# The last half tile of a matmul–GELU–matmul kernel stored in three pieces instead of two

## The chip, the cores and the metric

The kernel runs on one core of one Trainium2 chip. A core has five engines that run their own instruction streams: PE (TensorE, matrix products), DVE (VectorE), ACT (ScalarE), POOL (GpSimd) and SP (SyncE), and 16 DMA engines that move data between HBM and the on-chip memory. Engines wait for each other and for transfers through semaphores. The metric is device time in microseconds (us), from repeated runs; a profile shows one execution, instruction by instruction.

## What is computed

```python
m, k, n, p = 1024, 1024, 2048, 1024        # a: m x k, b: k x n, c: n x p, all float32

def reference(a, b, c):
    h = np.matmul(a, b)
    h = 0.5 * h * (1 + np.tanh(np.sqrt(2 / np.pi) * (h + 0.044715 * h ** 3)))
    return np.matmul(h, c).astype(np.float32)
```

## The kernel before

The products are made in tiles of 128 rows by 512 columns; one such float32 result fills one of the eight PSUM banks. Inputs are cast to bf16. The first product fills `hT` (the GELU of `a @ b`, transposed), partly with plain products and partly with a scheme of seven products in place of eight (a Strassen–Winograd form, class `Seven`, function `seven`); the sums that this scheme needs are made by DVE and kept in float32r. The second product, `h @ c`, is the call `seven(two, done2, between2)`: the output's 8 row tiles by 2 column halves are 16 tiles of 128x512, and each is stored as soon as it is complete.

The order of all instructions is written out by hand (`manual_schedule`): each engine runs its instructions in the order in which the program issues them. What matters here is the end of `seven` for `two`:

- The three output tiles (0,0,j), j = 0 to 2, are finished early, after the second group of products. `done2` stores them; those with j = 1 and j = 2 are stored in two halves of 256 columns each (line 436), the one with j = 0 whole.
- Then come the tiles (1,1,j) and (0,1,j) (function `p3`) and (1,0,j) (function `p4`; DVE copies these out of PSUM on line 434). Each is one store of 128x512, 256 KB.
- The tile (0,0,3) was left over: its first part `p1[3]` has lain in SBUF since the start of this stage, and its second product is made last of all, in lines 368 to 376. It is made in two halves of 256 columns. For each half, PE runs 8 matmuls (`w.product`, line 212, each with its own weight load) into a bank of its own (`bank(PY[i])`, where `PY` is `(7, 4, 5, 6)`), DVE adds `p1[3]` (line 375) into a piece `ot` of the pool "e", which has two buffers, and `store` (line 429) sends it to HBM.
- All stores and the five first loads are issued on SP's queue; the casting loads are issued on POOL's. ACT issues no transfer at all.

Transfers issued on hardware queues (SP's, and ACT's if it were used) take eight semaphores in turn, and each waits until the transfer eight places earlier has landed. There are 5 loads and 19 stores, 24 in all. After the last store is issued, SP waits for the eight semaphores one after the other, and a barrier of all engines ends the program.

Of the kernel before, what the change touches and what calls it, by code (L numbers as in the profile page):

```python
# [9 lines left out]
F32 = mybir.dt.float32  # L10
# [9 lines left out]
def kernel(ctx, tc, a, b, c, out):  # L20
    nc = tc.nc
# [21 lines left out]
    def bank(i, shape=(128, H), dt=F32, name="ps"):  # L43
        return pp.tile(list(shape), dt, name=name, tag=f"bank{i}", padded_shape=None)

    def pieces(tag, bufs, shape, dt, name):
        return small.tile(shape, dt, name=name, tag=tag, bufs=bufs)
# [248 lines left out]
    def snap(tag, p, name):  # L296
        st = pieces(tag, 4, [128, H], F32, name)
        nc.scalar.activation(st, p, AF.Copy)  # L298
        return st

    def plus(p, st):
        ot = pieces("o", 4, [128, H], F32, "ot")
        nc.vector.tensor_tensor(out=ot, in0=p, in1=st, op=ADD)  # L303
        return ot

    def seven(w, done, between):

        (A11, A12), (A21, A22) = w.A
        (B11, B12), (B21, B22) = w.B
        J = range(w.n)  # L310
        PX = X[:w.n]
        P2, PY = (X[2:], Y[:2]) if w.n == 2 else (Y, Y)
        if w is two:
            PY = (7, 4, 5, 6)
        px = [bank(i) for i in PX]
        p1, v, u, p2 = {}, {}, {}, []
        for j in J:
            w.product(px[j], A11, B11, j, True)
            if w is two and j == 3:
                p1[j] = pieces("ab", 2, [128, H], F32, "p1")  # L320
                nc.scalar.activation(p1[j], px[j], AF.Copy)
            else:
                p1[j] = snap("m", px[j], "p1")
        between("P1")
        for j in J if w is not two else range(3):
            p = bank(P2[j])
            w.product(p, A12, B21, j, True)
            if w.n == 2:
                p2.append(p)
            else:  # L330
                done(0, 0, j, plus(p, p1[j]))
        between("P2")
        py = [bank(i) for i in PY]
        for j in J:
            w.product(py[j], w.s[0], w.t[0], j, True)
        between("P5")
        for j in J:
            w.product(px[j], w.s[1], w.t[1], j, False)
            v[j] = snap("v", px[j], "v")
        between("P6")  # L340
        c22 = []
        for j in J:
            w.product(px[j], w.s[2], w.t[2], j, False)
            u[j] = snap("m", px[j], "u")
            c22.append(plus(py[j], u[j]))
            between(f"P7{j}")

        def p3(first):
            for j in J:
                if first:  # L350
                    done(1, 1, j, c22[j])
                w.product(py[j], w.last_s, w.t[3], j, False)
                done(0, 1, j, plus(py[j], v[j]))
            between("P3")

        def p4(first):
            for j in J:
                if first:
                    done(1, 1, j, c22[j])
                w.product(px[j], w.s[3], w.last_t, j, False)  # L360
                done(1, 0, j, px[j])

        for i, f in enumerate((p4, p3) if w.n == 2 else (p3, p4)):
            f(i == 0)
            if i == 0:
                for j, p in enumerate(p2):
                    done(0, 0, j, plus(p, p1[j]))
        if w is two:

            for i in range(2):  # L370
                r = ds(i * 256, 256)
                p = bank(PY[i])
                w.product(p, A12, B21, 3, True, i * 256, 256)
                ot = pieces("e", 2, [128, 256], F32, "ot")
                nc.vector.tensor_tensor(out=ot, in0=p[:, r], in1=p1[3][:, r], op=ADD)  # L375
                store(3, i * 256, 256, ot)


    two = Seven(8, [[hT[0][:, 0:8], hT[0][:, 8:16]], [hT[1][:, 0:8], hT[1][:, 8:16]]],
# [35 lines left out]
    zero.s1()  # L415
    zero.s2()
    seven(zero, done0, between0)
    one.s[3] = slot("b1", [128, 2, 4, H], F32R, "x1")[:, 0]
    one.s1()
    one.s2()  # L420
    seven(one, done1, between1)


# [4 lines left out]
    def store(mt, q0, w, ot, eng=None):  # L428
        (eng or nc.sync).dma_start(out=out[ts(mt, 128), ds(q0, w)], in_=ot)

    def done2(i, l, j, p):
        if (i, l) == (1, 0):
            ot = pieces("o", 4, [128, H], F32, "ot")
            nc.vector.tensor_copy(ot, p)
            p = ot
        n = 2 if (i, l) == (0, 0) and j else 1
        for q in range(n):
            r = ds(q * (H // n), H // n)
            store(4 * i + j, l * H + q * (H // n), H // n, p[:, r])

    def between2(n):
# [12 lines left out]
        elif n == "P73":  # L454
            two.t4(two.t[1], 4)

    seven(two, done2, between2)


# [28 lines left out]
```

## Time and profile before

| what | value |
|---|---|
| median of 3 runs | 117.73 us (117.45 to 117.9) |
| span of the profiled execution, first to last instruction | 115.67 us, granted TensorE clock 1.000 |
| own time of the profiled execution | not listed separately; the runs' median is 2.06 us above the span |
| PE, DVE, ACT, POOL busy | 111.1, 90.0, 51.4, 17.2 us |
| last instruction of PE / of DVE's arithmetic | ends at 112.4 / 112.9 us |
| last store issued on SP | 112.90 us |
| stores issued on SP's queue | 19 of `ot`: 13 of 256 KB, 6 of 128 KB |

Times in a timeline are counted from the span's start. A line of the timeline gives the start, the length, the engine, the line of the kernel, the operation, its tiles as output<-input, the shape, how many instructions were merged, and in brackets how long the engine had been idle and what ended that. "SPq" is SP's sequencer issuing a transfer; the transfer itself runs later on the DMA engines. A matmul's length contains its way through the array, so that successive matmuls overlap; the distance between their starts is what each one costs. "To landing" is the time from the start of an issue to the last semaphore update of that transfer.

### The profile page before, as it was taken

How to read it: one execution, taken by the hardware profiler on the slowest of the kernel's cores; microseconds unless marked ns; L12 is line 12 of the kernel's file. 1: busy time of each engine (PE TensorE's matmuls, PEld its weight loads, DVE VectorE, ACT ScalarE, POOL GpSimd, SP SyncE). 2: the span in 40 equal slices, each digit the busy share in tenths (PEclk: the TensorE clock that was granted, in tenths of full speed). 3: DMA queues.
4: the chain of work that ended last, by engine and by line, in shares of the span. 5: the costliest groups of instructions: out<-in, count | busy, mean ns of one | idle time of the engine just before them, and what ended most of it. 6: DMA issues, size and time to landing. Idle time of an engine off the chain costs nothing.

```text
span 115.7 us, 1461 instructions
## 1 busy us (share of the span) xinstructions
PE 111.1 (96%) x542; PEld 77.1 (67%) x542; DVE 90.0 (78%) x107; ACT 51.4 (44%) x86; POOL 17.2 (15%) x29
## 2 busy tenths in 40 slices
PE   7989999999999999999999999999999999999980
PEld 6645555546776447888885444688888888888860
DVE  0347748789999998935699999999999986954770
ACT  5053000999259997166698429500124982000000
POOL 2497755223322000000000000000000000000000
PEclk9999999999999999999999999999999999999999
DMA  2999999999999999998000000060000002014993
GB/s 69 295 381 229 200 199 205 204 208 205 206 211 209 212 213 209 212 210 168 8 0 0 6 0 0 38 235 0 0 0 0 0 4 91 1 73 176 370 363 106
DMA packets 13414, 15.94 MB, mean 138 GB/s; under 512 B 736, under 2 KB 9312, under 8 KB 13408
## 3 DMA queue, kind: packets, MB, share of 16 engines
q0 software_dynamic: 8672, 9.31, 47.6%
q1 hardware_dynamic: 4736, 6.56, 15.8%
q8 instruction: 4, 0.07, 0.3%
q14 instruction: 2, 0.02, 0.0%
HBM read 20.97 MB, written 4.19 MB: 218 GB/s over the span
## 4 chain that ended last, share of the span: by engine, by line
PE 90%; DMA 5%; SPq 1%; DVE 1%; issue 0%
PE ps L212 76%; PE ps L114 11%; DMA sta<-in_a_dram 5%; PE pt L145 3%; SPq L76 0%; DVE ab L110 0%; SPq L75 0%; DVE ot L375 0%
## 5 line engine op out<-in xcount | busy, mean ns | idle before, releaser
L212 PE MATMUL ps<-x,s 128*128 128x512 f32 x128 | 29.6, 391 | 0.0
L212 PEld LDWEIGHTS ps<-x,s 128*128 128x128 f32 x128 | 24.0, 188 | 5.1
L212 PE MATMUL ps<-x,x 128*128 128x512 f32 x96 | 22.9, 394 | 0.0
L212 PEld LDWEIGHTS ps<-x,x 128*128 128x128 f32 x96 | 18.0, 188 | 3.9
L114 PE MATMUL ps<-aT,b 128*128 128x512 bf16 x64 | 16.1, 379 | 0.2 <-DVE b L110 0.2
L298 ACT ACTIVATE v<-ps 128x512 f32<-128x512 f32 x10 | 6.0, 599 | 19.1 <-PE ps L212 19.1
L212 PE MATMUL ps<-c_sb,hT 128*128 128x512 bf16 (+1 forms) x72 | 14.2, 356 | 0.0
L212 PE MATMUL ps<-x 128*128 128x512 f32 x56 | 13.2, 392 | 0.0
L212 PEld LDWEIGHTS ps<-x 128*128 128x128 f32 x56 | 10.2, 188 | 2.6 <-ACT u L298 0.4
L118 ACT ACTIVATE hT<-ps 128x512 bf16<-128x512 f32 x14 | 7.3, 595 | 9.7 <-PE ps L114 9.7
L212 PEld LDWEIGHTS <-hT 128*128 128x128 bf16 x72 | 6.9, 98 | 7.0 <-issue 0.5
L118 ACT ACTIVATE hT<-ot 128x512 bf16<-128x512 f32 x18 | 10.4, 624 | 2.0 <-DVE ot L303 2.0
L212 PE MATMUL ps<-aT,b 128*128 128x512 bf16 x48 | 10.7, 379 | 0.0
L146 DVE COPY aT<-pt 128x512 bf16<-128x512 bf16 x16 | 6.7, 423 | 5.1 <-PE pt L145 5.1
L303 DVE TENSOR_TENSOR ot<-ps,u 128x512 f32<-128x512 f32 x10 | 6.7, 690 | 5.1 <-ACT u L298 5.1
L303 DVE TENSOR_TENSOR ot<-ps,v 128x512 f32<-128x512 f32 x10 | 6.7, 688 | 4.8 <-DMA out_dram<-ot 3.8
L170 DVE TENSOR_TENSOR x<-c_sb 128x1024 fp32r<-128x1024 bf16 x8 | 9.3, 1226 | 0.0
L114 PEld LDWEIGHTS <-b 128*128 128x128 bf16 x64 | 5.7, 98 | 4.5 <-DVE b L110 0.3
L212 PEld LDWEIGHTS <-b 128*128 128x128 bf16 x48 | 4.6, 98 | 5.7 <-issue 0.3
L104 POOL DMA_DIRECT2D c_sb<-in_c_dram x8 | 5.6, 702 | 13.1 <-DMA b<-in_b_dram 12.4
L170 DVE TENSOR_TENSOR x<-b 128x1024 fp32r<-128x1024 bf16 (+1 forms) x4 | 7.0, 1752 | 0.6 <-issue 0.6
L298 ACT ACTIVATE u<-ps 128x512 f32<-128x512 f32 x10 | 5.9, 598 | 3.4 <-PE ps L212 3.2
(44 smaller groups left out, 111.3 us busy)
## 6 DMA issues: line engine op xcount, KB each, us to landing
c_sb<-in_c_dram POOLq DMA_DIRECT2D x8, 512.0 KB, 20.0
out_dram<-ot SPq DMA_DIRECT2D x13, 256.0 KB, 2.1
b<-in_b_dram POOLq DMA_DIRECT2D x6, 512.0 KB, 15.3
sta<-in_a_dram SPq DMA_DIRECT2D x3, 512.0 KB, 6.1
abq<-in_a_dram POOLq DMA_DIRECT2D x5, 256.0 KB, 7.9
out_dram<-ot SPq DMA_DIRECT2D x6, 128.0 KB, 2.0
stb<-in_b_dram SPq DMA_DIRECT2D x1, 512.0 KB, 5.3
b<-in_b_dram POOLq DMA_DIRECT2D x2, 256.0 KB, 8.2
```

Of the source, the lines that this page charges most:

```text
L104: nc.gpsimd.dma_start(out=c_sb[:, t:t + 2], in_=cv[:, t:t + 2])
L114: nc.tensor.matmul(p, b1[:, k, ts(t, 128)], aT[:, h, k], start=(k == 0), stop=(k == KT - 1))
L118: nc.scalar.activation(hT[h][:, t], p, AF.Gelu_apprx_tanh)
L145: nc.tensor.transpose(pt[:, n, ts(m, 128)], ab[:, m, ts(n, 128)], ident)
L146: nc.vector.tensor_copy(aT[:, h, 2 * q + n], pt[:, n])
L170: nc.vector.tensor_tensor(out=dst[:, r], in0=x[:, r], in1=y[:, r], op=op)
L212: nc.tensor.matmul(p[:, ds(c0, w)], l[:, k, ts(j, 128)], r[:, k, ds(c0, w)], start=(start and k == 0), stop=(k == self.kt - 1), skip_group ...
L298: nc.scalar.activation(st, p, AF.Copy)
L303: nc.vector.tensor_tensor(out=ot, in0=p, in1=st, op=ADD)
```

## The change

The last half tile's second half is cut into two pieces of 128 columns. The pieces are now 256, 128 and 128 columns wide, each with 8 matmuls into a bank of its own (7, 4 and 5), one DVE addition and one store. The pool "e" gets a third buffer. The first piece's store is issued on ACT's queue, the other two on SP's. The early tile (0,0,2) is stored whole, so that there are still 24 transfers on the hardware queues (5 loads, 19 stores).

```diff
         if w is two:
-            for i in range(2):
-                r = ds(i * 256, 256)
+            for i, (c0, n) in enumerate(((0, 256), (256, 128), (384, 128))):
+                r = ds(c0, n)
                 p = bank(PY[i])
-                w.product(p, A12, B21, 3, True, i * 256, 256)
-                ot = pieces("e", 2, [128, 256], F32, "ot")
+                w.product(p, A12, B21, 3, True, c0, n)
+                ot = pieces("e", 3, [128, 256], F32, "ot")[:, 0:n]
                 nc.vector.tensor_tensor(out=ot, in0=p[:, r], in1=p1[3][:, r], op=ADD)
-                store(3, i * 256, 256, ot)
+                store(3, c0, n, ot, nc.sync if i else nc.scalar)
...
-        n = 2 if (i, l) == (0, 0) and j else 1
+        n = 2 if (i, l, j) == (0, 0, 1) else 1
         for q in range(n):
             r = ds(q * (H // n), H // n)
             store(4 * i + j, l * H + q * (H // n), H // n, p[:, r])
```

## The prediction

> **What bounds the kernel now.** I read the busy shares first, then the chain of waits, then the last microseconds line by line, since the change touches only those and one early store. From the page and the chain in order of time:
>
> ```profile
> PE 111.1 (96%) x542; PEld 77.1 (67%) x542; DVE 90.0 (78%) x107; ACT 51.4 (44%) x86; POOL 17.2 (15%) x29
> ...
> 24.46 87.96 PE ps L212 x400
> 112.42 0.02 issue
> 112.44 0.42 DVE ot L375
> ```
>
> PE is busy without a hole to 112.4 us; one DVE addition follows. From there on no engine computes, yet the span goes on to 115.7: a tail of 3.3 us of which the chain, which ends at the last computing instruction, shows only the beginning. The timeline of the end:
>
> ```profile
> 110.49 1.92 PE L212 MATMUL ps<-c_sb,hT 128*128 128x256 bf16 x16
> 110.68 0.69 DVE L434 COPY ot<-ps 128x512 f32<-128x512 f32 x1 [0.21 <-PE ps L212]
> 111.57 0.42 DVE L375 TENSOR_TENSOR ot<-ps,p 128x256 f32<-128x256 f32 x1 [0.20 <-PE ps L212]
> 112.44 0.42 DVE L375 TENSOR_TENSOR ot<-ps,p 128x256 f32<-128x256 f32 x1 [0.45 <-PE ps L212]
> ...
> 112.02 0.33 SPq L429 DMA_DIRECT2D out_dram<-ot  x1
> 112.90 0.33 SPq L429 DMA_DIRECT2D out_dram<-ot  x1
> ```
>
> Each addition starts some 0.04 us after its last matmul, each store some 0.03 us after its addition. The issues in the window from 111 us take this long to land, and the DMA engines' busy tenths from 113 to 114 and from 114 to 115 us (slices of 25 ns) show where the last one's data move:
>
> ```profile
> DMA to landing us min/median/max: 1.9/1.9/2.0
> ...
> DMA  9898999977441000000000000000053997999899
> ...
> DMA  9948541000000000000000000000000000000000
> ```
>
> The second burst is the last store: it begins in the slice at 113.73, 0.83 us after the issue, moves for 0.45 us to 114.18, and lands at about 112.90 + 1.88 = 114.78 (1.9 in the row, 1.88 by its last semaphore update). The barrier takes 115.67 - 114.78 = 0.89 us more. So the tail is: PE ends 112.41; addition to 112.87; issue 112.90; start 0.83; data 0.45; landing 0.60; barrier 0.89.
>
> **The change, part by part.**
>
> *PE.* Eight matmuls of 256 columns become sixteen of 128, with eight more weight loads. The old ones start every (1.92 - 0.27)/15 = 0.110 us (0.273 is the length of one), eight take 0.88. The new shape stands in the trace, with a weight load of the same shape before each: the transposes.
>
> ```profile
> 8.38 0.62 PE L145 MATMUL pt<-ident,ab 128*128 128x128 bf16 x8
> L145 PE MATMUL pt<-ident,ab 128*128 128x128 bf16 x24 | 2.2, 219 | 0.4 <-DVE aT L146 0.2
> ```
>
> (0.62 - 0.22)/7 = 0.057 us apart, sixteen 0.91. So +0.03 at most; from below 0 (the streamed columns are the same). I take +0.02. The Trainium skill, "TensorE: Matmul & The Clock Gate", section "Back-to-back issue gap", speaks against the change: it gives about 81 ns per matmul for a stream of load-and-multiply pairs at 128 columns. By that figure the sixteen would take an estimated 1.30 us, 0.42 more than now, and the sum below would end some 0.2 above the time before. This case's rows have 57 ns for such pairs, so the measurement decides. The third piece's bank was last read by the third addition of line 303, which ended at 106.24; PE comes to it at 111.8: 5.6 us of cover.
>
> *DVE.* The last addition shrinks from 256 to 128 columns, and another goes before it. The length by width:
>
> ```profile
> L303 DVE TENSOR_TENSOR ot<-ps,v 128x512 f32<-128x512 f32 x10 | 6.7, 688 | 4.8 <-DMA out_dram<-ot 3.8 <-PE ps L212 0.9
> L375 DVE TENSOR_TENSOR ot<-ps,p 128x256 f32<-128x256 f32 x2 | 0.8, 425 | 0.6 <-PE ps L212 0.6
> L110 DVE CAST b<-stb 128x128 bf16<-128x128 f32 x2 | 0.4, 225 | 0.5 <-DMA stb<-in_b_dram 0.5
> ```
>
> (688 - 425)/256 = 1.03 ns per column, so 425 - 132 = 293 ns; bounds 225 (the cast of that width) and 425 (no gain). The middle piece is ready on PE at about 111.98, its addition starts at 112.01 when DVE has done the first (112.00), ends 112.30; the last starts at 112.45 + 0.02 and ends at 112.76. The last addition gains 0.13 us (0 to 0.20). Three additions need three buffers and have them; none waits for a store.
>
> *Issue.* The middle store is issued at 112.33, the last at 112.79 if SP is free. Issues that follow one another directly are slower than the 0.33 of a lone one:
>
> ```profile
> 102.73 0.81 SPq L429 DMA_DIRECT2D out_dram<-ot  x2
> 105.67 1.81 SPq L429 DMA_DIRECT2D out_dram<-ot  x4
> ```
>
> 0.40 to 0.45 us each. From 112.33 SP is free at 112.73 to 112.78: just in time, so 0 (+0.01 at most). With the first store still on SP the three would go at 112.02, 112.47 and 112.92 by the longer spacing, and the 0.13 of DVE would be gone. That is what ACT's queue can be worth: 0 to 0.13. Its cover: ACT's last instruction before it ends at 96.84 and nothing but the barrier stands behind its wait.
>
> ```profile
> 96.24 0.60 ACT L298 ACTIVATE u<-ps 128x512 f32<-128x512 f32 x1 [1.21 <-PE ps L212]
> ```
>
> The Trainium skill, "DMA: Bandwidth & Descriptors", section "Queues, rings and completion order", says that SP and ACT each own a row of rings but no descriptor generator of their own. If the spacing of 0.45 us is that shared part's and not SP's, ACT's queue frees nothing and by this rule the 0.13 is lost; no row here has an issue on ACT.
>
> *Bytes.* The last store carries 64 KB in rows of 512 B in place of 128 KB in rows of 1 KB. By the burst, half of the data go: 0.45/2 = 0.22 at most. By landing times (page: median 2.1 us at 256 KB, 2.0 at 128 KB) 128 KB are worth 0.1, so 64 KB 0.05. I take 0.10, nearer the landing row, since it holds the acknowledgement too. The middle store's burst, 113.16 to some 113.4, is over when the last one's begins at 113.62; the first store's, on ACT's queue, runs from about 112.85 to 113.3.
>
> *ACT's queue, first use.* The first store has slack: issued at 112.02, it may take up to about 2.5 us (to 114.55) before it is last. SP's first issue of the program is the nearest row for an unused queue: 0.44 in place of 0.33 us, its data moving from the 100 ns slice at 1.8, so 1.1 us after the issue rather than 0.83. The store would then land after 1.9 + 0.3 = 2.2 us, at 114.2: hidden, with 0.3 us to spare. Its bounds are 1.9 (a store on SP) and 4.5 us (the longest store of the trace, issued at 94.55).
>
> *The early store.* One issue of 0.33 to 0.45 us less on SP at 75.6 us. The three stores of that place land by 78.0, and the additions that take their buffers again begin at 93.8, so it is hidden twice over. The count of transfers stays, so each late transfer waits for one eight places earlier: the last for a store issued near 109.2 and landed by 111.3. Worth 0.
>
> *Sum.* 0.13 + 0.10 - 0.02 - 0.01 = 0.20 us off the span, 115.67 to 115.47. The runs' median is 2.06 above this span; nothing on that side is touched by the rows, so 117.73 - 0.20 = 117.53. Bounds: gain of 0.02 (no DVE gain, 0.05 for bytes, -0.03 PE) to 0.42 (0.20 + 0.22), 117.71 to 117.31. Half a per cent of 117.73 is 0.59 us, about what a measurement of this kernel can tell from no change: even the best bound stays inside it.
>
> **The rivals.**
>
> *Small gain, as summed.* For it: every row of the tail. Chance 0.60, 117.53, own range 117.2 to 117.8 with the scatter of the three runs before.
>
> *No gain: issues share one part.* Three issues 0.45 us apart from 112.02 put the last at 112.92; only the bytes are left, less PE's 0.02: 117.65. For it: slow neighbouring issues; against: nothing measured on two queues. Chance 0.13.
>
> *Slower: ACT's first store lands last.* One mechanism: a queue that nothing has used becomes the end of the program. It sets the end from 2.5 us to landing, costs against before from 2.76 (114.78 - 112.02), and by over 0.5% from 3.35. At 3.5 us the time is 117.73 + 0.74 = 118.47; at the 4.5 us of the longest row 119.47. For it: one row shows such a latency, and no row has ACT issuing; against: the 18 other stores land in 1.9 to 2.6 us, and SP's first issue lost only 0.3. Chance 0.19.
>
> *Outside the span.* A second hardware queue could change the 2.06 us around the span, either way; no row bounds it but that total. Chance 0.08, with 117.2 to 118.4.
>
> **How the numbers follow.** The likeliest is 117.5. Slower by over 0.5%: 0.16 of the ACT case and half of the case outside the span, 0.20. Faster by over 0.5%: half of the latter, and a best-bound gain of 0.4 met by the runs' own scatter of 0.2: 0.10. Within: 0.70. The range goes from 117.1 (best bound less scatter) to 118.4 (the ACT case at 3.5 us).
>
> **What would show it.** Right: the pairs on PE 0.055 to 0.06 us apart; additions of 0.29 us; the last issue on SP between 112.75 and 112.80; its burst some 0.25 us long; landing near 114.57; the ACT store landed before that. Wrong: an ACT issue whose landing is the last, a last issue at 112.9 or later, pairs at 0.08 us, or a span that agrees while the runs don't.

## The result, and the profile after

| kernel | median of the runs | ratio to before, 95% interval |
|---|---|---|
| before | 117.6 us (22 runs, 117.4 to 118.05) | 1 |
| after | 117.24 us (22 runs, 117.04 to 117.86) | 0.9975 (0.9963 to 0.9987) |

The change is faster by a quarter of a per cent, 0.29 us by the ratio and 0.36 by the medians. The interval leaves out 1, and the gain lies inside the half per cent that the prediction took as its bound. The forecast was a gain of 0.20 us and 117.5.

The profiled execution after is one of the slower ones (117.6 us), and its span, 115.8, is longer than that of before. The chain in order of time of the changed kernel shows where:

```profile
24.87 2.81 PE ps L212 x13
```

Line 212, which fills the chain from there to the last addition, starts 0.41 us later than the 24.46 of before. What stands ahead of it are the first loads and products, which the change does not touch. So the spans can't be compared. What can be is the tail, from the end of PE's last matmul to the end of the span. The view of busy times by stretch (stretch, its length, busy time of PE, PE's weight loads, DVE, ACT and POOL with their counts, granted clock, DMA share, GB/s) has it, first for before:

```profile
112.41:115.67 3.26, 0.00 (x0) 0.00 (x0) 0.42 (x1) 0.00 (x0) 0.00 (x0) 1.00 0.38 140
```

and for the changed kernel:

```profile
112.89:115.82 2.93, 0.00 (x1) 0.00 (x0) 0.29 (x1) 0.00 (x0) 0.00 (x0) 1.00 0.48 166
```

3.26 us have become 2.93: 0.33 less. The timeline of the changed kernel shows the pieces:

```profile
110.95 1.94 PE L212 MATMUL ps<-c_sb,hT 128*128 128x256 bf16 x24
112.03 0.74 DVE L375 TENSOR_TENSOR ot<-ps,p 128x256 f32<-128x256 f32 x2
112.49 0.38 ACTq L429 DMA_DIRECT2D out_dram<-ot  x1
112.80 0.33 SPq L429 DMA_DIRECT2D out_dram<-ot  x1
112.93 0.29 DVE L375 TENSOR_TENSOR ot<-ps,p 128x128 f32<-128x128 f32 x1 [0.15 <-PE ps L212]
113.25 0.39 SPq L429 DMA_DIRECT2D out_dram<-ot  x1
```

The last addition takes 0.29 us in place of 0.42, the first store is issued on ACT at 112.49, and the two on SP go at 112.80 and 113.25, each some 0.03 after its addition. The last issue took 0.39 rather than 0.33; it follows another on the same queue by 0.45 us, and the experiments below show that this goes with such a neighbour. The landing times, of ACT's store and then of the last:

```profile
DMA to landing us min/median/max: 2.0/2.0/2.0
...
DMA to landing us min/median/max: 1.7/1.7/1.7
```

ACT's store landed at 112.49 + 1.99 = 114.49, the last at 113.25 + 1.70 = 114.94: the first use of ACT's queue was hidden with 0.45 us to spare. The DMA busy tenths of the changed kernel from 114 to 115 us, in slices of 25 ns:

```profile
DMA  6521015678999865210000000000000000000000
```

The middle store's data run out in the first slices, the last store's move from 114.14 to 114.48, 0.34 us against 0.49 before, both counted from the first packet's start to the last one's end.

| part of the tail, us | before | after | difference |
|---|---|---|---|
| PE's end to the last issue | 0.489 | 0.355 | -0.134 |
| issue to first packet | 0.833 | 0.895 | +0.062 |
| data moving | 0.490 | 0.341 | -0.149 |
| end of data to landing | 0.557 | 0.459 | -0.098 |
| landing to the end of the span | 0.893 | 0.883 | -0.010 |
| sum | 3.262 | 2.933 | -0.329 |

The second row is the longer issue: in both kernels the data begin 0.50 us after the issue's end (0.833 - 0.332 and 0.895 - 0.394).

### The profile page after: what moved, and what is told of

The parts are those of the page before. It is cut to its first block, busy times and chain, and to the rows that moved or that the text cites. A ratio compares the mean times of both kernels' runs of the same rounds, so it can differ in the third digit from the quotient of the medians.

```text
span 115.8 us, 1473 instructions
## 1 busy us (share of the span) xinstructions
PE 110.7 (96%) x544; PEld 77.1 (67%) x550; DVE 90.1 (78%) x108; ACT 51.4 (44%) x86; POOL 17.3 (15%) x29
## 4 chain that ended last, share of the span: by engine, by line
PE 79%; DMA 13%; POOL 5%; issue 0%; DVE 0%
PE ps L212 76%; DMA abq<-in_a_dram 10%; DMA sta<-in_a_dram 3%; POOL abq L86 3%; PE ps L114 2%; POOL b L89 1%; POOL gate L81 1%; PE pt L145 1%; POOL b L92 0%; DVE ot L375 0%
## 5 line engine op out<-in xcount | busy, mean ns | idle before, releaser
L114 PE MATMUL ps<-aT,b 128*128 128x512 bf16 x62 | 15.7, 379 | 0.3 <-DVE b L110 0.2
L212 PE MATMUL ps<-c_sb,hT 128*128 128x512 bf16 (+2 forms) x78 | 14.1, 336 | 0.1
L212 PE MATMUL ps<-aT,b 128*128 128x512 bf16 x46 | 10.6, 379 | 0.1
```

The source lines that it names most:

```text
L114: nc.tensor.matmul(p, b1[:, k, ts(t, 128)], aT[:, h, k], start=(k == 0), stop=(k == KT - 1))
L212: nc.tensor.matmul(p[:, ds(c0, w)], l[:, k, ts(j, 128)], r[:, k, ds(c0, w)], start=(start and k == 0), stop=(k == self.kt - 1), skip_group ...
```

## Experiments

Twelve kernels ran. Since the first loads scatter by several tenths of a microsecond from one execution to the next, the tail of each profile is the sharper measure; the ratio is to the kernel before on the same chip.

| kernel | tail, us | median, us | ratio (95% interval) |
|---|---|---|---|
| changed kernel again | 2.93 | 117.21 | 0.9982 (0.9966 to 0.9997) |
| all three stores on SP | 3.12 | 117.43 | 0.9996 (0.9987 to 1.0005) |
| middle store on ACT | 2.90 | 117.23 | 0.9958 (0.9929 to 0.9986) |
| last store on ACT | 3.01 | 117.3 | 0.9977 (0.9965 to 0.9988) |
| two additions, one store | 3.15 | 117.5 | 0.9999 (0.999 to 1.0008) |
| changed, early tile split: 25 transfers | 3.39 | 117.67 | 1.0017 (1.0006 to 1.0028) |
| before, early tile whole: 23 | 3.29 | 117.56 | 0.9997 (0.9986 to 1.0007) |
| before, first half on ACT | 3.26 | 117.56 | 1.0002 (0.9993 to 1.0011) |
| changed, 32 transfers | 2.89 | 117.32 | 0.9971 (0.9958 to 0.9985) |
| changed, 28 transfers | 3.17 | 117.54 | 0.9998 (0.9985 to 1.001) |
| pieces of 256, 160, 96 | 3.03 | 117.3 | 0.9977 (0.9964 to 0.9989) |
| last piece of 128 at an odd place | 3.00 | 117.25 | 0.9983 (0.9956 to 1.0009) |

**The control.** The changed kernel unaltered.

> The changed kernel again, as the control of these runs. The tail is the time from the end of PE's last matmul to the end of the span: 3.26 us before (112.41 to 115.67), 2.93 after (112.89 to 115.82). Theory (addition 0.13 shorter, last store 0.19 shorter from issue to landing): tail 2.93, ratio to before 0.997 to 0.998. Rival (the difference of the two profiles' tails is chance): tail anywhere between 2.9 and 3.3.

Tail 2.93 again, with its parts within 0.01 us of the table above. So the 0.33 between the tails is not the scatter of one profile.

**All three stores on SP.**

```diff
-                store(3, c0, n, ot, nc.sync if i else nc.scalar)
+                store(3, c0, n, ot)
```

> All three last stores on SP's queue. Theory: issues that follow one another on SP are 0.40 to 0.45 us apart, so that with the first at 0.40 us before PE's end the middle one goes at 0.00 to 0.05 after it and the last at 0.40 to 0.50 rather than at 0.36; tail 2.98 to 3.08, ratio to before 0.998 to 0.999. Rival (ACT's queue buys nothing, the gain is all in the cut): tail 2.93, ratio as the changed kernel's.

The tail came to 3.12, more than either end. The timeline of this kernel (PE ends at 112.55):

```profile
112.14 0.33 SPq L429 DMA_DIRECT2D out_dram<-ot  x1
112.57 0.41 SPq L429 DMA_DIRECT2D out_dram<-ot  x1
112.58 0.29 DVE L375 TENSOR_TENSOR ot<-ps,p 128x128 f32<-128x128 f32 x1 [0.15 <-PE ps L212]
113.07 0.41 SPq L429 DMA_DIRECT2D out_dram<-ot  x1
```

The last addition is done at 112.88, the last issue goes at 113.07. The three issues are 0.43 and 0.50 us apart, the second more than the 0.40 to 0.45 that was reckoned with. ACT's queue is worth 0.19 us of the 0.33. The cut alone keeps 0.14 in the tail, which the ratio of these runs can't tell from nothing.

**The middle store on ACT.**

```diff
-                store(3, c0, n, ot, nc.sync if i else nc.scalar)
+                store(3, c0, n, ot, nc.scalar if i == 1 else nc.sync)
```

> The middle store on ACT's queue, the first and the last on SP's, so that no issue on SP follows another directly. In the changed kernel the last issue took 0.394 us and its data began 0.895 after it, against 0.332 and 0.833 for the lone one before. Theory (the 0.06 is SP's own, for an issue right behind another on it): data again 0.83 after the issue, tail 2.87. Rival (the 0.06 comes with any three issues so close, whichever the queue): tail 2.93. A third: ACT's middle store lands last; it would have to take over 2.5 us.

The last issue took 0.333, as a lone one does, and its data began 0.85 us after it: 0.04 of the 0.06 came back, and the tail was 2.90. So the longer issue goes with a neighbour on SP's own queue; one on ACT's, 0.44 us ahead here, does not bring it. Against the control the runs show no difference (117.23 and 117.21), and the ratios' intervals overlap. Whether this placing is better stays open, at 0.03 us.

**The last store on ACT.**

```diff
-                store(3, c0, n, ot, nc.sync if i else nc.scalar)
+                store(3, c0, n, ot, nc.scalar if i == 2 else nc.sync)
```

> The last store on ACT's queue, the first two on SP's: the first transfer that ACT ever issues is now the one that the end waits for. Theory (ACT's first issue costs 0.377 in place of 0.332, as it did in the changed kernel, and nothing more): data 0.88 after the issue, tail 2.92. Rival (the first use of a queue costs 0.3, as on SP at the start of the program): data 1.1 to 1.2 after the issue, tail 3.1 to 3.2, near the time before.

The issue took 0.372, data began 0.90 after it, and it landed in 1.70, as the changed kernel's last store on SP does. So the first transfer that ACT issues costs 0.04 us more than a lone issue on SP and 0.07 up to its data, not 0.3. The tail is nevertheless 0.08 longer than the control's; 0.06 of that is one final wait of SP's that came after the landing at 114.54. For line 483, where the program ends, the view by source line has two of SP's semaphore waits from 114.52 to 114.65 us:

```profile
L483 SPq EVENT_SEMAPHORE  x2: 28/28/28, 114.6 to 114.6; - x2
```

The first of the two is the wait for this landing. In this kernel the last store raises the seventh of the eight semaphores and SP's middle store the eighth; the runs on the count of transfers show what that does.

**Two additions, one store.**

```diff
-                ot = pieces("e", 3, [128, 256], F32, "ot")[:, 0:n]
+                if i < 2:
+                    half = pieces("e", 3, [128, 256], F32, "ot")
+                ot = half[:, ds(c0 - 256, n)] if i else half
...
-                store(3, c0, n, ot, nc.sync if i else nc.scalar)
+                if i != 1:
+                    store(3, 256 if i else 0, 256, half, nc.sync if i else nc.scalar)
```

> The second half is still added in two pieces of 128 columns, but both go out in one store of 256 columns (128 KB) on SP; the first half stays on ACT. This leaves the shorter addition and takes the smaller store away. Theory (the two gains add up: 0.13 addition, 0.19 store): tail 3.26 - 0.13 = 3.13. Rival (the gain is the smaller store's alone): tail 3.26. Other rival (it is the earlier issue alone): tail 2.93 to 2.95.

The issue came 0.36 after PE's end, as early as in the changed kernel, and the store took 1.85 to land, as long as before; the tail was 3.15, 0.06 of it again one final wait behind the landing (this kernel has 23 transfers). Without that wait it would be 3.09, 0.17 below before and 0.16 above the changed kernel. The two gains do add up: 0.13 from the addition, and about 0.16 from the smaller store, which lands in 1.70 instead of 1.85.

**The early tile split again.**

```diff
-        n = 2 if (i, l, j) == (0, 0, 1) else 1
+        n = 2 if (i, l) == (0, 0) and j else 1
```

> The changed kernel with the early tile (0,0,2) stored in two halves again: 25 transfers on the hardware queues. Theory (the early store is hidden and the count of transfers costs nothing): tail 2.93, ratio as the changed kernel's. Rival (a 25th transfer shifts the turns of the eight semaphores so that one of the last stores waits for one that is late): the last issue later than 0.36 us after PE's end and a longer tail.

The theory fell. The tail was 3.39 and the kernel was slower than before the change (1.0017). Yet the last store was issued 0.36 us after PE's end and landed in 1.72: the rival as it was put, a late issue, is wrong too. The time is behind the landing. For line 483 the view by source line counts SP's semaphore waits, each shown as 0.028 us long, from 114.5 to 115.0 us in this kernel:

```profile
L483 SPq EVENT_SEMAPHORE  x8: 28/28/28, 114.6 to 115.0; - x8
```

and from 114.9 to 115.02 in the changed kernel:

```profile
L483 SPq EVENT_SEMAPHORE  x1: 28/28/28, 115.0 to 115.0; - x1
```

SP waits for the eight transfer semaphores in a fixed order. Transfers take the semaphores in turn, so that the 24th raises the eighth, and SP's wait for it is the last. The 25th raises the first: SP stands at its first wait until the last landing at 114.54, and then takes the seven others, all long fulfilled, one after the other, some 0.06 us each, 0.43 in all, before the barrier can begin. The other 0.03 of the 0.46 that the tail grew by is a landing 0.03 later. The view of SP's waits says the same: in this kernel the end waits for transfers once, for 1.3 us.

**Before, with only the early tile whole.** The same line edited in the kernel before.

> The kernel before with only the early tile (0,0,2) stored whole: 23 transfers. Theory: hidden, tail 3.26, ratio 1.000. Rival (that store's issue or the count matters): ratio off 1 by more than its interval.

Ratio 0.9997, so the early store itself costs nothing that can be told. The tail was 3.29; SP had one wait, 0.06 us, behind the last landing, as 23 transfers end on the seventh semaphore.

**Before, with only the first half on ACT.**

```diff
-                store(3, i * 256, 256, ot)
+                store(3, i * 256, 256, ot, nc.sync if i else nc.scalar)
```

> The kernel before with only the first half's store on ACT's queue. Theory: the last issue on SP was free before (0.88 us after the one ahead), so nothing is gained: tail 3.26, ratio 1.000. Rival (a second hardware queue costs or saves something in the tail or around the span): ratio off 1 with the tail unchanged, or another tail.

Tail 3.26, ratio 1.0002 (0.9993 to 1.0011): a second hardware queue by itself neither costs nor saves anything that these runs can tell (the interval is 0.1 us to either side), in the span or around it.

**32 and 28 transfers.** The changed kernel with the early tiles stored in smaller pieces; nothing at the end of the program is touched.

```diff
-        n = 2 if (i, l, j) == (0, 0, 1) else 1
+        n = 4 if (i, l) == (0, 0) else 1              # 32 transfers
+        n = (4, 2, 2)[j] if (i, l) == (0, 0) else 1   # 28 transfers
```

> The changed kernel with all three early tiles stored in four pieces of 128 columns: 12 early stores in place of 4, 32 transfers in all. With 25 transfers the tail grew to 3.39 us, while 24 had 2.93. Theory (what counts is which of the eight semaphores the last store raises: SP waits for them in a fixed order at the end, some 0.06 us each, so that all waits behind the last store's come after its landing; with 24 and 32 it is the last of the eight): tail 2.93, ratio as the changed kernel's, for all its eight transfers more. Rival (each transfer above 24 costs): tail over 3.39.

> The changed kernel with the early tiles stored in 4, 2 and 2 pieces: 28 transfers. Theory (order of the final waits): the last store raises the fourth semaphore, four waits of 0.06 us stand behind it, tail 2.93 + 0.25 = 3.18, between those of 24 and 25 transfers. Rival (each transfer above 24 costs, the first one 0.46): tail over 3.39, and over that with 32.

Both as the order of the waits has it. With 32 the tail is 2.89 and the ratio 0.9971, as good as with 24; with 28 it is 3.17. The same count of SP's waits, for 28 transfers from 114.75 to 115.05 us (the last landing was at 114.77):

```profile
L483 SPq EVENT_SEMAPHORE  x5: 28/28/28, 114.8 to 115.0; - x5
```

Five with the one that had been waiting: four too many. From 23 to 32 transfers it isn't their number that counts, only on which of the eight semaphores the last one ends.

**A smaller last piece.** Cuts of 256, 160 and 96 columns, the middle on ACT.

```diff
-            for i, (c0, n) in enumerate(((0, 256), (256, 128), (384, 128))):
+            for i, (c0, n) in enumerate(((0, 256), (256, 160), (416, 96))):
...
-                store(3, c0, n, ot, nc.sync if i else nc.scalar)
+                store(3, c0, n, ot, nc.scalar if i == 1 else nc.sync)
```

> Cuts of 256, 160 and 96 columns, the middle store on ACT's queue, first and last on SP's. Theory (addition 0.03 shorter, 16 KB less in the last store): tail 2.90 of the kernel with the middle store on ACT, less 0.03 and less 0.02 to 0.05: 2.82 to 2.85. Rival (rows of 384 B are written at a cost per row, or matmuls of 96 columns come no faster than those of 128): tail 2.90 or more, or PE's end later by up to 0.1.

The addition shrank to 0.26 and the last issue came 0.32 after PE's end, 0.03 earlier, as expected; the line 212 stretch at the end was no longer than in the changed kernel (1.94 us), so the matmuls did come faster with their width. But this last store took longer to land than the one of 128 columns, in the view by source line of this kernel (ACT's and the last store, then of the kernel with the middle store on ACT):

```profile
DMA to landing us min/median/max: 1.8/1.9/1.9
```

```profile
DMA to landing us min/median/max: 1.7/1.8/1.9
```

The last store is the minimum in each: 1.83 against 1.65. Its data took 0.32 us, hardly less than 0.34, and 0.65 us passed from their end to the landing, against 0.46. The tail was 3.03 and by it the smaller piece lost; the ratios can't tell. The Trainium skill, "DMA: Bandwidth & Descriptors", section "Specifications", gives 512 B as the least transfer for full rate and says that below it the engines read, modify and write; rows of 384 B that land later agree with that in direction, but no run here shows the cause. The cuts changed more than the rows: ACT's middle store grew to 80 KB and went out only 0.27 us ahead of the last one, so its data still moved until 113.80, while the last one's began at 113.64. With 128 columns the two overlapped by 0.02 us, not 0.16.

**The odd start.** Columns 160 to 287 as the last piece: 512 B rows, at a start that is no multiple of 256 B.

```diff
-            for i, (c0, n) in enumerate(((0, 256), (256, 128), (384, 128))):
+            for i, (c0, n) in enumerate(((0, 160), (288, 224), (160, 128))):
```

with the middle store on ACT as above.

> The last half tile's pieces in another order and size: columns 0 to 159 (SP), 288 to 511 (ACT), and last 160 to 287 (SP): the last store has rows of 512 B again, but each starts 640 B into its half of the output row, no multiple of 512 or of 256 B, as the rows of 384 B did (1664 B in). With 96 columns in the last store the data stopped about 0.65 us before the landing, with 128 columns 0.46. Theory (rows under 512 B are acknowledged later): tail 2.90, as with 128 columns and the middle store on ACT. Rival (it was the odd start): tail 3.05 or more.

Tail 3.00, between the two; 0.52 us from the end of the data to the landing, between 0.46 and 0.65. Inconclusive: landings of the same store scatter by nearly 0.1 (1.64 with 32 transfers, 1.69 in the control, 1.72 with 25). The middle store, 112 KB here, again overlapped with the last by 0.16 us, so this run does not leave that rival out. The width, the start and the neighbour's data may each have a part.

## Why the prediction was right

**What bounds.** Right: the gain lies wholly in the tail behind PE, and the table of its parts accounts for it.

**PE.** Forecast 0.057 us apart, measured 0.056 (the sixteen took from 111.83 to 112.89, the last being 0.22 long); eight pairs of before took 0.87, the sixteen 0.89. The +0.02 was right, and the figure of 81 ns for 128 columns does not hold for this stream.

**DVE.** 0.290 us measured for the last addition, 0.292 for the middle one, against 0.293 forecast; the gain up to the issue 0.134 against 0.13.

**Bytes.** This term was mis-sized: 0.10 was taken, 0.185 measured (issue to landing 1.880 to 1.695). The data took 0.15 less and the acknowledgement 0.10 less, and 0.06 went back at the start. The choice between the ends of 0.05 and 0.22, nearer the medians of the landing times, was the step that erred: what those medians, 256 against 128 KB, give per KB does not carry down to 64. They are also medians over the whole trace, with four stores of 128 KB issued in a row at 75 us, which landed in 1.94 to 2.10. The last stores of before alone, 2.03 to 2.09 at 256 KB against 1.88 to 1.89 at 128, would have given 0.14 to 0.21 for that halving. The burst, too, was read short: 0.45 off the slices where the packets have 0.49, and some 0.25 forecast where 0.34 was measured.

**Issue.** "Just in time" held on SP: the last issue waited for its addition, not for SP. What was missed is that a close neighbour on the same queue makes the issue 0.06 longer and its data that much later. The worth of ACT's queue was put at 0 to 0.13; the runs show 0.19 in the tail, as three issues in a row on SP are 0.43 and 0.50 apart. The spacing of 0.45 was a mean that hid this: the row of four issues at 105.67 has them 0.38, 0.52 and 0.46 apart. The rival in which both queues share the slow part of an issue fell: ACT's issue at 112.49 and SP's at 112.80 stand 0.31 apart, and SP's took 0.33 like a lone one.

**ACT's first use.** The slower rival fell: the store landed in 1.99 us, and it could have taken 2.45 before it was the last, and the last store on ACT showed a first use that is 0.04 us longer in the issue and lands as soon as SP's. The 0.3 taken from SP's first issue at the start of the program did not carry over. For the rival outside the span the ratio of 1.0002 (0.9993 to 1.0011) leaves no more than about 0.1 us.

**The early store.** Its own cost is nothing that can be told, as forecast. The reading of the wait in front of the last issue was off: the transfer eight places ahead of the last in the trace of before was issued at 106.57 and landed at 109.06, not 109.2 and 111.3; it was early either way. But the prediction weighed the count of transfers only against the waits in front of the late issues, and so missed what it does: with the early tile split, the 25th transfer would have cost 0.43 us of final waits at the very end (the tail grew by 0.46), more than the whole change gains. That this term came out as 0 is luck as far as the prediction goes: the change keeps 24, and the reason given for its being worth nothing was incomplete.

The sum: -0.33 in the tail and +0.02 on PE make -0.31, with -0.29 by the ratio, for -0.20 forecast; the size that was off is the bytes'.

## What to carry to other kernels

The time behind the last computing instruction is a sum of its own: last addition, issue, transfer, final waits, barrier; a smaller last piece shortened the addition and the transfer here, down to 128 columns and no further, as long as its issue did not queue behind its neighbours', which a second queue prevented. Count what stands behind the last landing: where the end waits for semaphores in a fixed order, let the last transfer end on the last of them. Compare such tails from PE's end in each trace, not by spans that scatter with the first loads.

## What had not been expected

- One transfer more at 75 us made the tail at 115 us 0.46 us longer, 0.43 of it by the order of the final waits; eight more cost nothing.
- The time from the end of the data to the landing is not fixed: for the last store it was 0.52 to 0.56 us with 1 KB rows, 0.41 to 0.49 with 512 B rows (0.52 at the odd start), and 0.65 with 384 B rows that start oddly. No run here separates row length from the store's size, and neither settles it alone: the middle stores, with the same 64 KB in 512 B rows, took 0.48 to 0.61.
- Issues in a row on SP slow each other (0.43, then 0.50 us apart), while an issue on ACT 0.31 us ahead leaves the length of SP's at 0.33.
